# A two-layer hybrid diffusion backbone on one core: half of the weights' low parts go to GpSimd, and the last modulation section is computed by rows on VectorE

## The chip, the cores and the metric

The kernel runs on one core of a Trainium2 chip. The metric is the device time of one execution in microseconds (us), taken as the median of several executions. The core has five engines with their own instruction streams: TensorE (PE, with its weight loads shown as PEld), VectorE (DVE), ScalarE (ACT), GpSimd (POOL) and SyncE (SP), which here only issues DMAs. Each engine runs its instructions in order; semaphores hold an instruction back until what it reads is there and what it overwrites is free.

## The reference

Two layers act on 256 latent tokens and 256 context tokens of width 1024. Each layer computes six modulation sections (shift, scale and gate, twice) from a condition vector, then three token mixers on one normalised input, a gated merge, and a squared-ReLU MLP. In the last layer only the latent tokens go through merge and MLP. Cut to what matters here:

```python
def reference(x, c, ctx, c_ctx, ...):
    h, hc = x, ctx
    for l in range(DEPTH):                                   # DEPTH = 2
        ctx_needed = l < DEPTH - 1
        sh1, sc1, gt1, sh2, sc2, gt2 = modulation(c, ada_w[l], ada_b[l])       # silu(c) @ w + b, in six sections
        sh1c, sc1c, gt1c, sh2c, sc2c, gt2c = modulation(c_ctx, ada_w[l], ada_b[l])
        u  = rms_norm(h,  norm1_g[l]) * (1.0 + sc1)  + sh1
        uc = rms_norm(hc, norm1_g[l]) * (1.0 + sc1c) + sh1c
        ya, yb, yc = ...          # recurrent block, gated linear recurrence, neighbourhood attention, all from u @ w_in[l]
        h = h + gt1 * merge_branches(ya, yb, yc, m_g, w_branch[l], w_out[l])
        h = h + gt2 * sq_relu_ffn(rms_norm(h, norm2_g[l]) * (1.0 + sc2) + sh2, ffn_w1[l], ffn_w2[l])
        if ctx_needed:
            hc = ...              # the same for the context
    return h
```

## The kernel before, in words

The two token streams lie side by side as 512 columns in layer 0. In layer 1 the context is only needed by some projections, and the rest works on 256 columns. Every matmul is done in a split format: a weight piece and its activations are each the sum of a high part and a low part, and three products (high by high, low by high, high by low; L240 to L242, L253 to L255, L272 to L275, L1073 to L1075) stand for one.

A layer has 148 weight pieces of 512 KB, 296 in all, which come in a fixed order. For each piece SP issues one DMA into `raw` (`arriving`, L208 to L212, 3 buffers), ScalarE casts the high part `whi` (L226), and VectorE subtracts it from `raw` to get the low part `wlo` (L227); there are 4 buffers each of `whi` and `wlo`. `fetch` near the end of the kernel starts a piece up to four pieces ahead of its use. The one exception before the change is the very first piece, whose low part is computed on GpSimd by the same line.

The time runs through these stages: a start (0 to about 60 us), four heads of the mixers in layer 0 (to about 390 us), the merge with the output projection (to about 585 us), a norm (`normed`, with lines L461 to L538), the MLP (to about 925 us), the layer boundary with the next norm, four heads in layer 1 (to about 1253 us), the merge of layer 1 (to about 1318 us), its output projection and norm (to about 1350 us) and the last MLP. Within a head the chains of small operations on VectorE and ScalarE (scores, scans, the chunked recurrence with `KK`, `QQ`, `lv`) lie beside the projections `ptok` on PE. In the merge the gates `gt` multiply the projected branches `halves`, and the sum `msum` is split into `mhi` and its low part, which the output projection reads. In a norm the sums of squares `sums` go through PE (`nss`), a short chain on VectorE gives the reciprocal root `r_g` (L531 to L538), PE spreads it (`rst`, L484), and VectorE and ScalarE make the operand `x` (L502 to L506) for the next projections. The residual stream is `h` (L1207).

The modulation sections other than the first two are computed by rows: for a section, 8 DMAs of 512 KB (`arow`) and 16 multiply-and-sum operations on VectorE (`junk`, L395), as lane "X" of the side work. The last section, (1,5), which is the gate after the last MLP, is the exception: `last_modulation` loads 8 blocks (`araw`), PE multiplies them in 32 fp32 matmuls (L419, 64 records in the trace), of which some are placed after output pieces and the rest in the norm of layer 1, and four small matmuls (L428) bring the result into its layout.

GpSimd does little else: constants, a rotary table (`ctab`, L367), and the issue of the DMAs for `bias` and `gw`. Lanes (L101 to L147) decide at each step of the main work which pieces of side work are issued beside it. The instructions of VectorE, ScalarE and GpSimd are put in order by the builder's list scheduler, so an instruction that leaves one engine can change the order of its neighbours.

Of the kernel before, what the change touches and what calls it, by code (L numbers as in the profile page):

```python
# [19 lines left out]
P = 128  # L20
# [7 lines left out]
HB = 64  # L28
# [5 lines left out]
}  # L34
ROW_SECTIONS = ((0, 2), (0, 3), (0, 4), (0, 5), (1, 0), (1, 1), (1, 2), (1, 3), (1, 4))
LAST_SECTION = (1, 5)
MIX_ORDER = ("tok", "ff", "fb", "hq", "ax", "ag", "og")
# [117 lines left out]
def hybrid_kernel(  # L155
    ctx: ExitStack, tc: tile.TileContext, xT, cT, wpack, ada0w, adaw, lastw, prm, lruw, biasd, consts, cs, gfr, masks, out
):
# [17 lines left out]
    def four_k(name, shape=(2, T2), dt=F32):  # L175
        return wk.tile([P] + list(shape), dt, tag="t4", name=name, bufs=N4)

    def psum(tag, name):
        return ps.tile([P, T2], F32, tag=tag, name=name, bufs=PSUM_BUFS[tag])
# [8 lines left out]
    con = cpool.tile([P, P + 1], F32, name="con")  # L188
    sel = cpool.tile([P, 10], F32, name="sel")
    cst = cpool.tile([P, 2, 2, 64], F32, name="cst")  # L190
# [181 lines left out]
    def modulation_rows():  # L372
# [16 lines left out]
        for i, (l, section, k) in enumerate(todo):  # L389
# [16 lines left out]
            yield 2.4, 1 if l or section == 5 else 0  # L406

    def last_modulation():

        l, section = LAST_SECTION  # L410
        raws = []
        for k in range(KD):
            raws.append(four_k("araw", (4, TL)))
            nc.sync.dma_start(out=raws[k], in_=lastw[k].rearrange("p (a b) -> p a b", b=TL))
            yield
        pa = psum("AV", "ada")
        for k in range(KD):
            for g in range(4):
                nc.tensor.matmul(  # L419
                    pa[32 * g:32 * g + 32, :TL], lhsT=cs32[:, k, :], rhs=raws[k][:, g], start=(k == 0), stop=(k == KD - 1)  # L420
                )
            yield
        sb = scr("adasb")[:, :TL]
        nc.vector.tensor_copy(sb, pa[:, :TL])
        yield 0.4, 2
        pt = psum("L", "adat")
        for m in range(2):
            nc.tensor.matmul(pt[:, 8 * m:8 * m + 8], lhsT=sb[:, m * P:(m + 1) * P], rhs=sel[:, 2:], start=True, stop=True)  # L428
        src = pt[:, :16].rearrange("p (m g s) -> p m g s", g=4, s=2)
        b = par(l, "ada_b")[:, section * 8:section * 8 + 8].rearrange("p (g m) -> p m g", g=4)  # L430
        for s in range(2):
            dst = section_of(l, section, s).rearrange("p (g m) -> p m g", g=4)
            nc.vector.tensor_tensor(out=dst, in0=src[:, :, :, s], in1=b, op=ALU.add)
        known.add(LAST_SECTION)

# [676 lines left out]
    def merge_pieces(l):  # L1112
# [73 lines left out]
        def pre_out():  # L1186
            st.u2 = new_u()
            new_sums()
            if l > 0:
                st.late = last_modulation()  # L1190

        def finished(d, s):
            square(d, s, l > 0)
            if l > 0:
                next(st.late)

# [52 lines left out]
    def ffn_pieces(l):  # L1249
# [6 lines left out]
        def open_ffn():  # L1256
            lanes.step("N")
            for _ in range(5):
                next(st.late)
            lanes.step("N")  # L1260
            for _ in range(3):
                next(st.late)
            lanes.start("X", st.late)

# [74 lines left out]
    def start():  # L1339
# [3 lines left out]
        nc.scalar.dma_start(out=con, in_=consts[:, :P + 1])  # L1343
        nc.scalar.dma_start(out=sel, in_=consts[:, P + 1:P + 11])
        for k in range(0, KD, 2):
# [90 lines left out]
        def later():  # L1436

            nc.sync.dma_start(out=prn[1], in_=prm[1][:, :NMOD])
            nc.sync.dma_start(out=cst, in_=cs)
            for l in range(DEPTH):  # L1440
                nc.sync.dma_start(out=gf[l], in_=gfr[l])
                for i in (0, 2):
                    nc.gpsimd.tensor_scalar_mul(gf[l][:, i], gf[l][:, i], 0.125)
            nc.sync.dma_start(out=idh, in_=consts[:, P + 11:])
            mskf = two_k("mskf").rearrange("p (a b) -> p a b", b=HB)[:, :NLEV]
            nc.sync.dma_start(out=mskf, in_=masks)
            nc.gpsimd.tensor_copy(msk, mskf)
# [30 lines left out]
    pos = [0]  # L1478

    def fetch(n):  # L1480
        while len(ready) < n and pos[0] < len(todo):
            l, key = todo[pos[0]]
            ready.append(weights(l, key))
            pos[0] += 1
# [15 lines left out]
def _lay(inputs):  # L1500
# [37 lines left out]
    a["adaw"] = np.concatenate([section(*i).T.reshape(KD, P, D) for i in ROW_SECTIONS])  # L1538
    a["lastw"] = section(*LAST_SECTION).reshape(KD, P, D)

# [36 lines left out]
    i = np.arange(P)  # L1577
    con = np.zeros((P, P + 11 + HB), np.float32)
    con[:, :P] = np.eye(P)
# [13 lines left out]
    a["gfr"] = np.broadcast_to(gr[:, None], (DEPTH, P, 4, 64))  # L1593
    for g in range(4):
        for s in range(2):
            con[:, P + 3 + 2 * g + s] = i == 32 * g + s
    con[:, P + 11:] = i[:, None] % HB == i[None, :HB]
    a["consts"] = con
# [7 lines left out]

_ORDER = ["xT", "cT", "wpack", "ada0w", "adaw", "lastw", "prm", "lruw", "biasd", "consts", "cs", "gfr", "masks"]

# [21 lines left out]
```

## Time and profile before

| | |
|---|---|
| time, median of 3 runs | 1532.23 us (1531.86 to 1532.8) |
| the profiled execution, its own time | 1530.86 us |
| its span in the trace | 1529.1 us |
| PE busy | 1509.4 us (99%) |
| DVE busy | 1167.3 us (76%) |
| ACT busy | 752.8 us (49%) |
| POOL busy | 26.6 us (2%) |
| low parts on DVE (L227, `wlo`) | 295, together 360.3 us |
| rows on DVE (L395, `junk`) | 144, together 173.3 us |

The page gives busy times of each engine over the whole span. A share is an average: PE is nearly always busy, but there are stretches in which it waits for VectorE, and others in which VectorE has time to spare. The stage windows and the timelines show which is which. In a timeline row the columns are start, duration, engine, line, operation, output and inputs, shape and count; in square brackets stands the idle time before the instruction and what ended it. A row with a count over 1 joins several instructions that followed each other.

### The profile page before, as it was taken

Reading aid. Unit: us, or ns where it says so; the run is one execution under the profiler, and the core shown is the slowest. Engines: PE = TensorE matmul, PEld = TensorE weight load, DVE = VectorE, ACT = ScalarE, POOL = GpSimd, SP = SyncE. Lnnn points to the kernel's source line nnn. Section 1 sums busy time; section 2 is a strip of 40 time slices with the busy share of each in tenths; the row PEclk is TensorE's granted clock in tenths of the full one; section 3 lists DMA queues with packets and bytes.
Section 4 is the critical chain, followed back from the end, with each engine's and each line's share of the span. In section 5 each row is a group of like instructions: output and inputs, shape, how many; then the busy total and the mean of one; then the engine's idle time right before and its main releaser. Section 6 shows DMA issues by size and latency. Waiting matters only on the chain.

```text
span 1529.1 us, 22454 instructions
## 1 busy us (share of the span) xinstructions
PE 1509.4 (99%) x8593; PEld 1247.9 (82%) x8594; DVE 1167.3 (76%) x2250; ACT 752.8 (49%) x1285; POOL 26.6 (2%) x57
## 2 busy tenths in 40 slices
PE   9999999999999999999999999999999999989998
PEld 5778787878888889888888888878878888778887
DVE  6777778686478898988695846779678878878886
ACT  3466575656323333532323323576776865444552
POOL 1100000020000000000000000000000000000000
PEclk9999999999999999999999999999999999989999
DMA  9413131222273661555464532414223356635553
GB/s 368 156 42 104 56 104 56 70 76 70 86 259 124 215 213 69 179 192 179 165 206 138 193 111 89 126 62 138 90 70 118 111 179 209 234 132 185 190 191 127
DMA packets 61788, 217.26 MB, mean 142 GB/s; under 512 B 7792, under 2 KB 9456, under 8 KB 61680
## 3 DMA queue, kind: packets, MB, share of 16 engines
q1 hardware_dynamic: 59328, 209.88, 40.1%
q0 software_dynamic: 1648, 5.77, 1.1%
q8 instruction: 68, 1.11, 0.3%
q14 instruction: 40, 0.33, 0.1%
q10 hardware_dynamic: 704, 0.17, 0.1%
HBM read 214.74 MB, written 1.05 MB: 141 GB/s over the span
## 4 chain that ended last, share of the span: by engine, by line
PE 94%; DVE 3%; issue 1%; ACT 1%; DMA 1%; SPq 0%; ACTq 0%
PE pd L240 5%; PE pd L242 5%; PE pd L241 5%; PE pd L275 4%; PE pf L275 3%; PE ptok L1073 3%; PE pf L240 3%; PE pf L241 3%; PE pf L242 3%; PE ptok L1074 3%; PE ptok L1075 3%; PE pg L240 3%; PE pg L242 3%; PE pg L241 3%; PE lv L590 2%; PE pd L273 2%
## 5 line engine op out<-in xcount | busy, mean ns | idle before, releaser
L226 ACT CAST whi<-raw 128x1024 fp32r<-128x1024 f32 x296 | 311.1, 1052 | 446.1 <-PE pd L241 111.8
L227 DVE TENSOR_TENSOR wlo<-raw,whi 128x1024 fp32r<-128x1024 f32 x295 | 360.3, 1224 | 107.0 <-ACT whi L226 101.9
L395 DVE CUSTOM_DVE_ANT_0 junk<-arow,crow 128x1024 bf16<-128x1024 f32 x144 | 173.3, 1220 | 1.5 <-DMA arow<-in_adaw 1.3
L1207 DVE SCALAR_TENSOR_TENSOR h<-pd,mod,h 128x256 f32<-128x256 f32 x160 | 73.7, 482 | 69.7 <-PE pd L242 51.1
L242 PE MATMUL pd<-hhi,wlo 128*128 128x512 f32 (+1 forms) x288 | 105.4, 366 | 0.0
L240 PE MATMUL pd<-hhi,whi 128*128 128x512 f32 (+1 forms) x288 | 105.3, 366 | 0.0
L241 PE MATMUL pd<-hlo,whi 128*128 128x512 f32 (+1 forms) x288 | 105.3, 366 | 0.0
L1073 PE MATMUL ptok<-whi,x 128*128 128x512 f32 (+1 forms) x224 | 86.9, 393 | 1.1 <-DVE h L1207 1.1
L241 PE MATMUL pf<-x,whi 128*128 128x512 f32 x224 | 87.2, 389 | 0.0
L240 PE MATMUL pf<-x,whi 128*128 128x512 f32 x224 | 87.2, 389 | 0.0
L242 PE MATMUL pf<-x,wlo 128*128 128x512 f32 x224 | 87.2, 389 | 0.0
L1074 PE MATMUL ptok<-whi,x 128*128 128x512 f32 (+1 forms) x224 | 85.1, 381 | 0.2 <-DVE x L506 0.2
L1075 PE MATMUL ptok<-wlo,x 128*128 128x512 f32 (+1 forms) x224 | 84.4, 377 | 0.0
L275 PE MATMUL pf<-x,whi 128*128 128x512 f32 x224 | 81.0, 402 | 0.0
L275 PE MATMUL pd<-hhi,whi 128*128 128x512 f32 x224 | 79.9, 396 | 0.0
L240 PE MATMUL pg<-x,whi 128*128 128x512 f32 x192 | 76.2, 397 | 0.0
L242 PE MATMUL pg<-x,wlo 128*128 128x512 f32 x192 | 74.9, 390 | 0.0
L241 PE MATMUL pg<-x,whi 128*128 128x512 f32 x192 | 74.8, 390 | 0.0
L273 PE MATMUL pf<-x,wlo 128*128 128x256 f32 x256 | 67.0, 284 | 0.0
L273 PE MATMUL pd<-hhi,wlo 128*128 128x256 f32 x256 | 66.1, 279 | 0.0
L242 PEld LDWEIGHTS pd<-hhi,wlo 128*128 128x128 f32 x288 | 54.3, 189 | 8.8
L241 PEld LDWEIGHTS pd<-hlo,whi 128*128 128x128 f32 x288 | 54.3, 189 | 8.8
(395 smaller groups left out, 3651.4 us busy)
## 6 DMA issues: line engine op xcount, KB each, us to landing
raw<-in_wpack SPq DMA_DIRECT2D x296, 512.0 KB, 3.3
arow<-in_adaw SPq DMA_DIRECT2D x72, 512.0 KB, 4.7
a<-in_ada0w SPq DMA_DIRECT2D x16, 512.0 KB, 10.3
araw<-in_lastw SPq DMA_DIRECT2D x8, 512.0 KB, 5.7
bias<-in_biasd POOLq DMA_DIRECT2D x7, 512.0 KB, 4.4
h<-in_xT SPq DMA_DIRECT2D x4, 512.0 KB, 5.5
gw<-in_lruw POOLq DMA_DIRECT2D x8, 256.0 KB, 3.0
out<-h SPq DMA_DIRECT2D x8, 128.0 KB, 1.9
```

Of the source, the lines that this page charges most:

```text
L226: nc.scalar.copy(hi, src)
L227: eng.tensor_tensor(out=lo, in0=src, in1=hi.bitcast(F32), op=ALU.subtract)
L240: nc.tensor.matmul(d, lhsT=whi[:, k, :], rhs=xhi, start=(k == 0), stop=False)
L241: nc.tensor.matmul(d, lhsT=whi[:, k, :], rhs=xlo, start=False, stop=False)
L242: nc.tensor.matmul(d, lhsT=wlo[:, k, :], rhs=xhi, start=False, stop=(k == nk - 1))
L273: nc.tensor.matmul(dst[:, :TL], lhsT=wlo[:, k, :], rhs=xk[:, 0], start=False, stop=False)
L275: nc.tensor.matmul(dst, lhsT=whi[:, k, :], rhs=xk, start=False, stop=last)
L395: nc.vector.tensor_tensor_reduce(out=junk, in0=raw, in1=crow[s], scale=1.0, scalar=0.0, op0=ALU.mult, op1=ALU.add, accum_out=section_of(l, ...
L1073: nc.tensor.matmul(dst, lhsT=xhi[:, k, tsl], rhs=whi[:, kk, :], start=(k == 0), stop=False)
L1074: nc.tensor.matmul(dst, lhsT=xlo[:, k, tsl], rhs=whi[:, kk, :], start=False, stop=False)
L1075: nc.tensor.matmul(dst, lhsT=xhi[:, k, tsl], rhs=wlo[:, kk, :], start=False, stop=(k == KD - 1))
L1207: nc.vector.scalar_tensor_tensor(out=h[:, d, sl], in0=p_[:, part], scalar=mods(l, section, s)[:, d:d + 1], in1=h[:, d, sl], op0=ALU.mult, ...
```

## The change

The low part of a weight piece is computed on GpSimd where the piece's position in the order is odd, and also for the first four pieces of the MLP (`f1`) in each layer; all others stay on VectorE. Together with the first piece these are 151 low parts on GpSimd and 145 on VectorE. The modulation section (1,5) joins the others in `ROW_SECTIONS`; `last_modulation`, its input `lastw` and its selection columns go away. Lane "N" (the norm) is then issued in one go when the MLP opens. Line numbers after the change are lower by 1 to 39.

```diff
-ROW_SECTIONS = ((0, 2), (0, 3), (0, 4), (0, 5), (1, 0), (1, 1), (1, 2), (1, 3), (1, 4))
-LAST_SECTION = (1, 5)
+ROW_SECTIONS = ((0, 2), (0, 3), (0, 4), (0, 5), (1, 0), (1, 1), (1, 2), (1, 3), (1, 4), (1, 5))
...
-    def last_modulation():
-
-        l, section = LAST_SECTION
-        raws = []
-        for k in range(KD):
-            raws.append(four_k("araw", (4, TL)))
-            nc.sync.dma_start(out=raws[k], in_=lastw[k].rearrange("p (a b) -> p a b", b=TL))
-            yield
-        pa = psum("AV", "ada")
-        for k in range(KD):
-            for g in range(4):
-                nc.tensor.matmul(
-                    pa[32 * g:32 * g + 32, :TL], lhsT=cs32[:, k, :], rhs=raws[k][:, g], start=(k == 0), stop=(k == KD - 1)
-                )
-            yield
...
             new_sums()
-            if l > 0:
-                st.late = last_modulation()
 
         def finished(d, s):
             square(d, s, l > 0)
-            if l > 0:
-                next(st.late)
...
         def open_ffn():
-            lanes.step("N")
-            for _ in range(5):
-                next(st.late)
-            lanes.step("N")
-            for _ in range(3):
-                next(st.late)
-            lanes.start("X", st.late)
+            lanes.flush("N")
...
+    def low_part_engine(key, i):
+
+        return nc.gpsimd if i % 2 or (key[0] == "f1" and key[1] == 0 and key[2] < 4) else nc.vector
+
     def fetch(n):
         while len(ready) < n and pos[0] < len(todo):
             l, key = todo[pos[0]]
-            ready.append(weights(l, key))
+            ready.append(weights(l, key, eng=low_part_engine(key, pos[0])))
             pos[0] += 1
```

On VectorE in the norm between merge and MLP of layer 0, the order before was this (`r_g` is the reciprocal root, `h` the residual stream, `sums` the sums of squares):

```order
L531 TENSOR_SCALAR r_g_5387<-nss 128x2
L532 TENSOR_SCALAR r_g_5387<-r_g_5387 128x2
L533 TENSOR_SCALAR r_g_5387<-r_g_5387 128x2
L227 TENSOR_TENSOR wlo<-raw,whi 128x1024
L538 SCALAR_TENSOR_TENSOR r_g_5387<-r_g_5387 128x2
L461 TENSOR_TENSOR sums<-sums,sqt 128x256
L538 SCALAR_TENSOR_TENSOR r_g_5387<-r_g_5387 128x2 x3
L1207 SCALAR_TENSOR_TENSOR h<-pd,mod_85,h 128x256
L538 SCALAR_TENSOR_TENSOR r_g_5387<-r_g_5387 128x2 x3
L227 TENSOR_TENSOR wlo<-raw,whi 128x1024
```

Now the same engine has this order at the same place:

```order
L502 TENSOR_SCALAR r_g_5387<-nss 128x2
L503 TENSOR_SCALAR r_g_5387<-r_g_5387 128x2
L504 TENSOR_SCALAR r_g_5387<-r_g_5387 128x2
L509 SCALAR_TENSOR_TENSOR r_g_5387<-r_g_5387 128x2 x2
L432 TENSOR_TENSOR sums<-sums,sqt 128x256
L509 SCALAR_TENSOR_TENSOR r_g_5387<-r_g_5387 128x2 x5
L1174 SCALAR_TENSOR_TENSOR h<-pd,mod_85,h 128x256
```

The low parts have gone from VectorE's chain here; they are on GpSimd, which has no other instruction between them.

On VectorE at the layer boundary, in front of the second norm chain, the order before was this:

```order
L502 SCALAR_TENSOR_TENSOR ut<-h,A_g_8206,rst 128x256
L461 TENSOR_TENSOR sums<-sums,sqt 128x256
L1207 SCALAR_TENSOR_TENSOR h<-pd,mod_85,h 128x256
L506 SCALAR_TENSOR_TENSOR x<-ut,mod_86,x 128x256
L227 TENSOR_TENSOR wlo<-raw,whi 128x1024
L461 TENSOR_TENSOR sums<-sums,sqt 128x256
L227 TENSOR_TENSOR wlo<-raw,whi 128x1024
L531 TENSOR_SCALAR r_g_8388<-nss 128x2
```

Now it is this, with rows of the modulation (L394) among them:

```order
L473 SCALAR_TENSOR_TENSOR ut<-h,A_g_8233,rst 128x256
L432 TENSOR_TENSOR sums<-sums,sqt 128x256
L394 ISA junk,mod_86<-arow,crow 128x1024
L394 ISA mod_86 128x1
L477 SCALAR_TENSOR_TENSOR x<-ut,mod_86,x 128x256
L394 ISA junk,mod_86<-arow,crow 128x1024
L394 ISA mod_86 128x1
L1174 SCALAR_TENSOR_TENSOR h<-pd,mod_85,h 128x256
L226 TENSOR_TENSOR wlo<-raw,whi 128x1024
L432 TENSOR_TENSOR sums<-sums,sqt 128x256
L502 TENSOR_SCALAR r_g_8420<-nss 128x2
```

One low part has gone from this chain, and two row operations have come in ahead of the residual.

On VectorE in the norm of layer 1, the order before was this, up to the chain of the reciprocal root:

```order
L227 TENSOR_TENSOR wlo<-raw,whi 128x1024
L1207 SCALAR_TENSOR_TENSOR h<-pd,mod_86,h 128x256 x2
L227 TENSOR_TENSOR wlo<-raw,whi 128x1024
L461 TENSOR_TENSOR sums<-sums,sqt 128x256
L1207 SCALAR_TENSOR_TENSOR h<-pd,mod_86,h 128x256 x2
L227 TENSOR_TENSOR wlo<-raw,whi 128x1024
L461 TENSOR_TENSOR sums<-sums,sqt 128x256
L1207 SCALAR_TENSOR_TENSOR h<-pd,mod_86,h 128x256
L531 TENSOR_SCALAR r_g_12378<-nss 128x2
```

Now it is this:

```order
L1174 SCALAR_TENSOR_TENSOR h<-pd,mod_86,h 128x256 x3
L432 TENSOR_TENSOR sums<-sums,sqt 128x256 x2
L1174 SCALAR_TENSOR_TENSOR h<-pd,mod_86,h 128x256 x2
L432 TENSOR_TENSOR sums<-sums,sqt 128x256
L1174 SCALAR_TENSOR_TENSOR h<-pd,mod_86,h 128x256 x2
L432 TENSOR_TENSOR sums<-sums,sqt 128x256
L1174 SCALAR_TENSOR_TENSOR h<-pd,mod_86,h 128x256 x2
L502 TENSOR_SCALAR r_g_12403<-nss 128x2
```

No low part stands on VectorE any more in the last steps ahead of the chain.

## Rows read from the trace of the kernel before

**Rows 1.** The page: busy times, and the chain that ended last.
```profile
PE 1509.4 (99%) x8593; PEld 1247.9 (82%) x8594; DVE 1167.3 (76%) x2250; ACT 752.8 (49%) x1285; POOL 26.6 (2%) x57
...
PE 94%; DVE 3%; issue 1%; ACT 1%; DMA 1%; SPq 0%; ACTq 0%
```

**Rows 2.** The page's costliest groups: low parts and rows on DVE.
```profile
L227 DVE TENSOR_TENSOR wlo<-raw,whi 128x1024 fp32r<-128x1024 f32 x295 | 360.3, 1224 | 107.0 <-ACT whi L226 101.9
L395 DVE CUSTOM_DVE_ANT_0 junk<-arow,crow 128x1024 bf16<-128x1024 f32 x144 | 173.3, 1220 | 1.5 <-DMA arow<-in_adaw 1.3
```

**Rows 3.** Timeline of POOL at the start: the one low part on GpSimd.
```profile
11.67 2.34 POOL L227 TENSOR_TENSOR wlo<-raw,whi 128x1024 fp32r<-128x1024 f32 x1 [11.23 <-ACT whi L226]
```

**Rows 4.** Timeline of DVE in the same microseconds.
```profile
11.32 0.17 DVE L342 TENSOR_TENSOR lq<-lq,lz 128x16 f32<-128x16 f32 x1
...
11.73 2.31 DVE L342 TENSOR_TENSOR lq<-lq,lz 128x16 f32<-128x16 f32 x1
```

**Rows 5.** Stage windows: busy time (count) by engine, granted PE clock, DMA share, GB/s.
```profile
60.00:390.00 330.00, 330.00 (x2144) 264.76 (x2143) 236.15 (x474) 208.17 (x388) 10.65 (x21) 1.00 0.22 74
...
625.00:925.00 300.00, 300.00 (x1327) 248.51 (x1325) 223.31 (x349) 92.46 (x121) 0.53 (x1) 1.00 0.50 171
...
1253.00:1320.00 67.00, 65.36 (x385) 54.12 (x386) 57.30 (x115) 37.93 (x75) 0.00 (x0) 1.00 0.63 220
1320.00:1350.00 30.00, 23.02 (x132) 18.83 (x131) 24.31 (x53) 12.80 (x23) 0.00 (x0) 0.83 0.43 140
```

**Rows 6.** Timeline of DVE in the norm of layer 0.
```profile
588.48 1.23 DVE L227 TENSOR_TENSOR wlo<-raw,whi 128x1024 fp32r<-128x1024 f32 x1
```

**Rows 7.** Timeline of PE at the first MLP matmul of layer 0.
```profile
594.34 0.62 PE L253 MATMUL pf<-x,whi 128*128 128x256 f32 x3 [0.49 <-ACT x L505]
```

**Rows 8.** Timeline of DVE at the layer boundary.
```profile
943.68 1.23 DVE L227 TENSOR_TENSOR wlo<-raw,whi 128x1024 fp32r<-128x1024 f32 x1
...
954.94 1.23 DVE L227 TENSOR_TENSOR wlo<-raw,whi 128x1024 fp32r<-128x1024 f32 x1
```

**Rows 9.** Timeline of PE at the layer boundary.
```profile
962.34 0.44 PE L1074 MATMUL ptok<-whi,x 128*128 128x384 f32 x1 [0.20 <-DVE x L506]
```

**Rows 10.** Windows of 10 us in the first head of layer 1.
```profile
1000.00:1010.00 10.00, 10.00 (x54) 7.75 (x52) 8.78 (x26) 7.45 (x16) 0.00 (x0) 1.00 0.29 99
1010.00:1020.00 10.00, 10.00 (x73) 7.58 (x74) 5.04 (x17) 7.88 (x16) 0.54 (x1) 1.00 0.04 9
```

**Rows 11.** Timeline of DVE at the end of the merge of layer 1.
```profile
1309.59 1.22 DVE L227 TENSOR_TENSOR wlo<-raw,whi 128x1024 fp32r<-128x1024 f32 x1 [0.21 <-ACT whi L226]
1310.73 0.42 DVE L230 SCALAR_TENSOR_TENSOR mhi<-msum,mhi 128x256 fp32r<-128x256 f32 x1
1311.06 0.41 DVE L300 TENSOR_TENSOR halves<-halves,pp 128x256 f32<-128x256 f32 x1
...
1312.88 0.42 DVE L230 SCALAR_TENSOR_TENSOR mhi<-msum,mhi 128x256 fp32r<-128x256 f32 x1 [0.48 <-ACT mhi L229]
```

**Rows 12.** Timeline of PE in the norm of layer 1.
```profile
1332.24 0.40 PE L275 MATMUL pd<-mhi,whi 128*128 128x512 f32 x1
1332.57 1.50 PE L419 MATMUL ada<-araw,cs 128*32 128x256 f32 x24
1336.72 0.38 PE L470 MATMUL nss<-con,sums 128*128 128x1 f32 x2 [2.65 <-DVE sums L461]
...
1342.95 0.76 PE L272 MATMUL pf<-x,whi 128*128 128x512 f32 x1 [1.84 <-DVE x L506]
```

**Rows 13.** Timeline of DVE in the same norm.
```profile
1332.86 1.22 DVE L227 TENSOR_TENSOR wlo<-raw,whi 128x1024 fp32r<-128x1024 f32 x1
...
1335.12 1.22 DVE L227 TENSOR_TENSOR wlo<-raw,whi 128x1024 fp32r<-128x1024 f32 x1
```

**Rows 14.** PE lines, by form: line, operation, count, busy us and mean ns.
```profile
L419 PE MATMUL ada<-araw,cs 128*32 128x256 f32 x64 | 4.9, 385 | 0.0
...
L428 PE MATMUL adat<-sel,adasb 128*128 128x8 f32 x4 | 0.5, 235 | 0.0
```

More of the change, by code (lines that the diff above doesn't have):

```diff
@@ L155, in hybrid_kernel @@
 def hybrid_kernel(
-    ctx: ExitStack, tc: tile.TileContext, xT, cT, wpack, ada0w, adaw, lastw, prm, lruw, biasd, consts, cs, gfr, masks, out
+    ctx: ExitStack, tc: tile.TileContext, xT, cT, wpack, ada0w, adaw, prm, lruw, biasd, consts, cs, gfr, masks, out
 ):
@@ L188, in hybrid_kernel @@
     con = cpool.tile([P, P + 1], F32, name="con")
-    sel = cpool.tile([P, 10], F32, name="sel")
+    sel = cpool.tile([P, 2], F32, name="sel")
     cst = cpool.tile([P, 2, 2, 64], F32, name="cst")
@@ L406, in modulation_rows @@
             yield 2.4, 1 if l or section == 5 else 0
-    def last_modulation():
-        l, section = LAST_SECTION
-        raws = []
-        for k in range(KD):
-            raws.append(four_k("araw", (4, TL)))
-            nc.sync.dma_start(out=raws[k], in_=lastw[k].rearrange("p (a b) -> p a b", b=TL))
-            yield
-        pa = psum("AV", "ada")
-        for k in range(KD):
-            for g in range(4):
-                nc.tensor.matmul(
-                    pa[32 * g:32 * g + 32, :TL], lhsT=cs32[:, k, :], rhs=raws[k][:, g], start=(k == 0), stop=(k == KD - 1)
-                )
-            yield
[L423 to L434, printed above, removed]
     known = {(0, 0), (0, 1)}
@@ L1343, in start @@
         nc.scalar.dma_start(out=con, in_=consts[:, :P + 1])
-        nc.scalar.dma_start(out=sel, in_=consts[:, P + 1:P + 11])
+        nc.scalar.dma_start(out=sel, in_=consts[:, P + 1:P + 3])
         for k in range(0, KD, 2):
@@ L1443, in later @@
                     nc.gpsimd.tensor_scalar_mul(gf[l][:, i], gf[l][:, i], 0.125)
-            nc.sync.dma_start(out=idh, in_=consts[:, P + 11:])
+            nc.sync.dma_start(out=idh, in_=consts[:, P + 3:])
             mskf = two_k("mskf").rearrange("p (a b) -> p a b", b=HB)[:, :NLEV]
@@ L1538, in _lay @@
     a["adaw"] = np.concatenate([section(*i).T.reshape(KD, P, D) for i in ROW_SECTIONS])
-    a["lastw"] = section(*LAST_SECTION).reshape(KD, P, D)
     pm = np.empty((DEPTH, P, NPRM), np.float32)
@@ L1577, in _lay @@
     i = np.arange(P)
-    con = np.zeros((P, P + 11 + HB), np.float32)
+    con = np.zeros((P, P + 3 + HB), np.float32)
     con[:, :P] = np.eye(P)
@@ L1593, in _lay @@
     a["gfr"] = np.broadcast_to(gr[:, None], (DEPTH, P, 4, 64))
[L1594 to L1597, printed above, removed]
+    con[:, P + 3:] = i[:, None] % HB == i[None, :HB]
     a["consts"] = con
@@ L1604, in _lay @@
     return {k: np.ascontiguousarray(v) for k, v in a.items()}
-_ORDER = ["xT", "cT", "wpack", "ada0w", "adaw", "lastw", "prm", "lruw", "biasd", "consts", "cs", "gfr", "masks"]
+_ORDER = ["xT", "cT", "wpack", "ada0w", "adaw", "prm", "lruw", "biasd", "consts", "cs", "gfr", "masks"]
 def build(nc, arrays):
```

## The prediction, made before the changed kernel ran

> **What bounds the kernel now.** I read the page first: busy times and the chain that ended last [rows 1]. PE is busy 99% of the span and holds 94% of the chain; VectorE is at 76%, GpSimd at 2%. So PE's own work sets the time, and VectorE matters only where PE waits for it or has it close behind. On average there is room for both edits; the average hides where it is not. The stage windows come second [rows 5]: in the heads of layer 0 VectorE works 236.15 of 330 us (72%) and in the MLP of layer 0 223.31 of 300 us (74%), while PE is busy throughout. In the merge of layer 1 VectorE has 57.30 of 67 us (86%) and PE loses 1.6 us; in the norm behind it PE is busy only 23.02 of 30 us. Timelines of the tight places come last [rows 6 to 13], and the start of the kernel, where GpSimd does once what it is now to do 151 times [rows 3, 4].
>
> **What a low part costs on either engine.** On VectorE it takes 1.22 us [rows 2]. On GpSimd it took 2.34 us, from 11.67 to 14.01 [rows 3]. In the same microseconds VectorE had a subtraction of 128x16, which takes 0.17 us a moment before; the one that began at 11.73 took 2.31 us and ended with GpSimd's [rows 4]. Both of its operands lie in SBUF, as do those of most of VectorE's work here. So while GpSimd computes a low part, VectorE can be held for all of it. A moved part then costs VectorE up to 2.31 - 1.22 = +1.09 us where VectorE has two-operand work ready, and gives 1.22 us where VectorE would have been idle or was reading PSUM. With 150 parts moved the ends are 150 x 1.09 = +163 us and 150 x 1.22 = 183 us less work for VectorE; neither is a change of the span, because PE covers most of both.
>
> The Trainium skill has a rule on this ("SBUF — State Buffer", section "Who interferes with whom"): GpSimd uses VectorE's second pair of SBUF ports, as an exclusive lock; a VectorE instruction with two SBUF inputs and a GpSimd instruction that reads SBUF shut each other out, and the one issued first holds the pair for its whole length. The 2.31 us beside the 2.34 us agree with it. By that rule the sum below stands as it is; with two engines that don't meet, it would be that of the first rival.
>
> **Part one, half of the low parts to GpSimd, stage by stage.**
>
> *MLP of both layers and the gate stretches of layer 0.* PE is busy without a gap and VectorE is at 74% [rows 5]. Every second piece moved adds 1.09 us of hold per two pieces at the worst; in the 300 us there are about 64 pieces, so 32 x 1.09 = 35 us on 223 us, 258 of 300. The buffers of four pieces carry the delay. I take 0; were the cover gone, the price could reach 35 us.
>
> *Norm of layer 0.* Four low parts of the first MLP pieces stood on VectorE; the one at 588.48 lies inside the chain of the reciprocal root, and the other three around it. All go to GpSimd. PE waited 0.49 us at the first matmul [rows 6, 7] and is paced by VectorE and ScalarE behind it. Bounds: all four hidden, 4 x 1.22 = -4.9; all four holding, 4 x 1.09 = +4.4. Two come while VectorE runs `x` without a pause: I take 2 x 1.09, and 0.3 for the rest: +2.5, near the upper end, since the nearest row of a collision [rows 4] is a full hold.
>
> *Layer boundary.* Two low parts, at 943.68 and 954.94, move [rows 8], and PE is paced by `x` from 962.34 on [rows 9]. Behind the first edit alone: -2.4 to +2.2. The second edit puts two row operations ahead of the residual of the second half, 2 x 1.22 = +2.4, and takes one low part away. I take +1.1 for one full hold and +1.9 for the rows, less what the removed part gives back: +3 together, of bounds 0 to +4.8.
>
> *Heads.* Five low parts per head move, 20 in a layer. In layer 0 a head lasts 330 / 4 = 82 us and VectorE has 28% to spare [rows 5], so I take 0 there. In layer 1 it is dense in parts, 8.78 of 10 us in one window and 5.04 in the next [rows 10]; the windows behind these are alike. PE's small matmuls of the recurrence have the chain close behind them. Of 20 moved parts I let 5 or 6 fall into dense stretches and pay in full: 5.5 x 1.09 = +6. The ends are -4 (all hidden, PE gaining nothing it does not wait for) and 20 x 1.09 = +21.8.
>
> *Merge of layer 1.* VectorE is the bound here, with PE waiting for `halves` and `mhi`. Of 18 low parts from 1257 us on, the last at 1309.59, nine move. `halves` reads PSUM and can run beside GpSimd (0.41 us), the others cannot; and there are idles of 0.48 us in which a moved part is free [rows 11]. About five of the nine pay 1.09 - 0.42 = 0.67 us: +3.4, say +3.5. Ends: 9 x 1.22 = -11 if nothing collided, of which PE could use only its 1.6 us of loss [rows 5], and 9 x 1.09 = +9.8.
>
> *Norm of layer 1.* The last projection matmul starts at 1332.24, yet PE waits 2.65 us for `sums` at 1336.72, because two low parts of 1.22 us stand between the last residuals on VectorE [rows 12, 13]. The order shows none there now. That is 2.4 us off the chain, of which I take -2.2 since a late GpSimd part may still hold the chain once. The clock was granted at 0.83 of full over these 30 us [rows 5], which is half for about 10 us (0.17 x 30 / 0.5), the level of 1.2 GHz; PE had been idle in the gap before. A gap that is 2 us shorter remains one, so I leave that fall in place.
>
> **Part two, the last section by rows.** Removed: 4.9 us of matmuls for the section, and 0.5 us for the four small ones [rows 14]. 24 of the 64 ran from 1332.57 on inside the gap in which PE waits anyway [rows 12], and the others between output pieces while PE waits for VectorE. So I count only the four small ones: -0.5, and at most -(4.9 - 1.5) - 0.5 = -3.9. Added: 16 row operations of 1.22 us [rows 2], 19.5 us on VectorE between about 880 us and the boundary, covered by PE (DVE 74% of that stage) but for the two counted there. Eight DMAs of 512 KB replace eight others; the DMA share is 0.50 there [rows 5], so nothing.
>
> **The sum.** 2.5 + 3 + 6 + 3.5 - 2.2 - 0.5 = +12.3 us on the profiled execution's 1530.86 gives 1543.2. That execution lies 1.37 us under the median of the runs shown (1532.23), so 1544.5; I say 1544.
>
> **Rivals.**
>
> 1. *GpSimd fits into VectorE's pauses and VectorE is relieved.* For it: VectorE idles 362 us in the span, and 74% and 72% leave room [rows 5]. Then the norm of layer 1 gives -2.2, the last section up to -3.9, and the loss of PE at the merge 1.6 at most: -7.7 at most, and about -6 with the section at its middle, so 1526. Against it: PE's waits sit where VectorE has no pause [rows 6, 11, 13], and there a hold of 2.31 replaces 1.22.
> 2. *Nothing to measure.* Holds and gains cancel within 3 us: the heads take no loss (-6 from the sum), the merge and the boundary half of theirs (-1.8 and -1.5): +3, or 1535; without the norm of layer 0 as well +0.5, or 1533. For it: PE is busy without a gap in both heads' stages. Against it: the same as against the first.
> 3. *VectorE becomes the bound in the heads of layer 1.* If each of its 20 moved parts pays in full, +21.8 takes the place of +6: 12.3 + 15.8 = +28.1, so 1560. It decides where holds raise VectorE from about 8.8 of 10 us to over 10: two moved parts in a dense window add 2.2 and do so [rows 10]. Against it: the windows between are half empty, and a delay can be caught up there.
> 4. *The other order of holding.* If VectorE gets in first, GpSimd's part waits instead and lands late, and PE waits for `wlo`. Then the price is on PE's weight side, in stretches where pieces are short; a part that comes one VectorE operation of 1.22 us later [rows 2] in each of the 20 places is +24 for +6, so 1563. Against it: four buffers lie between a low part and its use.
>
> **How the numbers follow.** Forecast 0.50 (1537 to 1553 as its own range), rival 1 0.17, rival 2 0.15, rival 3 0.12, rival 4 0.06. The likeliest gives 1544. The range must reach into rivals 1 and 3 so that about 2 in 10 stay outside: 1527 to 1562. 0.2% of the time is 3.1 us, about what can be told from no change here. Faster by more (under 1529.1): rival 1 and a trace of rival 2, 0.18. Within it: most of rival 2, 0.12. Slower: the rest, 0.70.
>
> **What would show it.** In the trace after, each GpSimd low part has 2.3 us, and VectorE rows of 0.4 us with two SBUF operands stretch to up to 2.3 beside it; single-operand rows and those reading PSUM do not. In the norm of layer 1 PE's wait for `sums` falls from 2.65 to about 0.5 us. At the matmuls that stood at 594 and 962 us, PE's waits for `x` grow by 2 to 3 us in all at each place. In the heads of layer 1 PE shows waits for `QQ`, `km` or `x` that it did not have. I am wrong if those rows on VectorE keep their old durations, or if they stretch and PE's stages keep their lengths; then VectorE's pauses are larger where it counts than I read them.

## The result, and the profile after the change

The change makes the kernel slower: 1587.92 us (median of 4 runs, 1586.81 to 1589.49) against 1532.51 us, a ratio of 1.0359 with a 95% interval of 1.0341 to 1.0377. The direction was forecast, the size was not: 55 us instead of 12, and outside the range of 1527 to 1562. (Executions of one kernel lie up to 7 us apart; in the profiles of spare_read, spare_write, two_kept, short_ops and rows_early the clock is granted low for a part of the first 30 us, and some or all of their entry under "start" in the table below comes from that.)

The page after the change answers to [rows 1, 2]: busy times, the chain that ended last, and the groups of low parts and rows (lines left out are marked by dots).

```profile
PE 1521.5 (96%) x8525; PEld 1250.2 (79%) x8526; DVE 1213.4 (77%) x2130; ACT 751.8 (47%) x1285; POOL 410.4 (26%) x207
...
PE 76%; DVE 18%; ACT 4%; issue 2%; DMA 0%; SPq 0%; DVEq 0%; ACTq 0%
...
L226 POOL TENSOR_TENSOR wlo<-raw,whi 128x1024 fp32r<-128x1024 f32 x151 | 385.5, 2554 | 1131.7 <-ACT whi L225 1105.9
...
L226 DVE TENSOR_TENSOR wlo<-raw,whi 128x1024 fp32r<-128x1024 f32 x145 | 180.0, 1242 | 61.4 <-ACT whi L225 60.2
L394 DVE CUSTOM_DVE_ANT_0 junk<-arow,crow 128x1024 bf16<-128x1024 f32 x160 | 215.9, 1366 | 1.4 <-DMA arow<-in_adaw 0.9
```

VectorE has given away 150 low parts, 183 us of work, and taken on 16 rows, 21 us. By this sum it should be busy 1005 us. It shows 1213.4, 46 us more than before: its operations have become longer. The share of the chain that lies on VectorE has grown from 3% to 18%. PE's idle time is 1585.0 - 1521.5 = 63.5 us, against 1529.1 - 1509.4 = 19.7 before, which is 43.8 of the 56 us. The other 12.1 us are time that the trace counts as busy on PE, although 5.4 us of matmuls have gone [rows 14]; a low clock has at most 8.5 us of it (see below), and the rest stays open. These waits of PE in the heads of layer 1 are new:

```profile
PE pr L861 <- DVE lx L226: 6.5, 4, 1.7
PE lv L599 <- DVE QQ L612: 5.5, 4, 1.6
PE sc L760 <- ACT PT L811: 1.4, 1, 1.4
PE pg L271 <- DVE halves L299: 1.1, 2, 0.7
```

These rows give what PE waited for, the total, how often and the longest. The first two come four times each, once in each head. Not one of them names GpSimd's `wlo`; in the whole trace one wait of PE does, of 0.5 us. What they look like, first on GpSimd, then on VectorE, then on PE, in the first head of layer 1 (timelines):

```profile
1025.36 2.38 POOL L226 TENSOR_TENSOR wlo<-raw,whi 128x1024 fp32r<-128x1024 f32 x1 [6.42 <-ACT whi L225]
1054.70 2.85 POOL L226 TENSOR_TENSOR wlo<-raw,whi 128x1024 fp32r<-128x1024 f32 x1 [26.97 <-ACT whi L225]
```

```profile
1026.09 1.93 DVE L946 SCALAR_TENSOR_TENSOR ge<-ge,halves 128x256 f32<-128x256 f32 x1
1027.94 0.41 DVE L772 TENSOR_REDUCE misc<-sc 128x1 f32<-128x256 f32 x1
1028.27 0.68 DVE L226 TENSOR_TENSOR lx<-xc,lx 128x512 fp32r<-128x512 f32 x1
...
1054.62 0.69 DVE L608 TENSOR_TENSOR KK<-KK,aux 128x512 f32<-128x512 f32 x1 [0.32 <-PE lv L561]
1055.23 2.60 DVE L612 TENSOR_TENSOR QQ<-QQ,aux 128x256 f32<-128x256 f32 x1
```

```profile
1029.00 0.74 PE L861 MATMUL pr<-lx,lw 128*128 128x512 f32 x2 [1.65 <-DVE lx L226]
...
1057.97 0.46 PE L599 MATMUL lv<-QQ,KK 128*128 128x128 f32 x2 [1.63 <-DVE QQ L612]
```

The operation on `ge` that starts at 1026.09 ends at 1028.02, after GpSimd's at 1027.74; `lx` comes behind it, and PE waits for `lx`. `QQ` takes 2.60 us, ends at 1057.83 after GpSimd's at 1057.55, and PE waits 1.63 us for it. Before, the same operation took 0.42 us:

```profile
L641 DVE TENSOR_TENSOR QQ<-QQ,aux 128x256 f32<-128x256 f32 x24 | 10.1, 420 | 6.0 <-PE lv L590 3.7 <-PE lv L629 2.3
```

To see where the 56 us of the span lie I paired PE's instructions of both traces by output tile and position, and took the shift of their starts at the stages' edges. Each column is what a stage adds, in us, against the profiled execution before; the experiments stand in the same table. One execution stands behind each line: in layer 0 two_kept and norm_vec have the order of instructions on VectorE that the change has as far as the end of the heads, and their heads read +12.3 and +11.0 beside +9.6, so that entries of this size are good to 2 or 3 us.

```
                start  heads 0  merge 0  norm 0  MLP 0  boundary  heads 1  merge 1  norm 1  MLP 1 |  sum
prediction        -       0        0      +2.5     0      +3.0      +6.0     +3.5     -2.7     0  | +12.3
the change      +1.8    +9.6     +1.5     +4.8     0      +7.0     +24.4     +3.6     +1.8   +1.5 | +56.0
rows_only       -0.6       0     +0.1        0     0      +4.1      -0.1     -0.3     -0.1      0 |  +3.2
gp_only         +1.4    +9.6     +1.5     +4.8     0      +3.0     +22.2     +4.3     +3.6   +1.3 | +51.6
spare_read      +4.0    +9.4     +2.9     +9.5     0      +3.9     +20.2    +12.6     +7.2   +7.7 | +77.4
spare_write     +4.9       0        0     +0.7     0         0         0     +5.4     -1.9      0 |  +9.1
zero_low        -0.6    -0.4     +0.1     -1.0     0      +5.1      +1.8     -3.1     -4.7      0 |  -2.8
two_kept        +3.2   +12.3     +1.6     +4.2     0      +7.9     +11.4     +5.2     +1.0   +1.5 | +48.3
short_ops       +2.1    +7.5     +1.6     +3.9     0      +7.6     +13.0     +0.2     +0.9      0 | +36.7
mlp_only           0    +0.1        0        0     0         0         0     +0.1     -0.2   +0.9 |  +0.8
rows_early      +4.9       0     +0.1     +1.3     0         0      -0.1     -0.3     +1.0      0 |  +6.8
zero_early      -1.1    -0.4     +0.1     -2.2     0      -0.3      +1.9     -2.6     -3.8      0 |  -8.5
norm_vec           0   +11.0     +1.5        0     0      +7.5     +22.7     +3.6     +1.4   +0.9 | +48.6
```

Two further places of the change. In layer 0 half of the heads' loss lies in one spot (+5.0 of 9.6): GpSimd, VectorE and PE there, with VectorE's `KK` before as the first of its rows,

```profile
338.09 2.40 POOL L226 TENSOR_TENSOR wlo<-raw,whi 128x1024 fp32r<-128x1024 f32 x1 [11.94 <-ACT whi L225]
```

```profile
330.02 0.69 DVE L637 TENSOR_TENSOR KK<-KK,blk 128x512 f32<-128x512 f32 x1
...
338.24 2.79 DVE L608 TENSOR_TENSOR KK<-KK,blk 128x512 f32<-128x512 f32 x1
340.96 0.41 DVE L772 TENSOR_REDUCE misc<-sc 128x1 f32<-128x256 f32 x1
```

```profile
344.82 1.12 PE L807 MATMUL tp<-con,s 128*128 128x128 f32 x4 [3.25 <-ACT s L783]
```

The held `KK` has the reduction of the attention scores behind it in VectorE's queue, ScalarE's exponential waits for that, and PE for ScalarE. In the norm of layer 1, which answers to [rows 12, 13], three low parts in a row on GpSimd hold `sums`:

```profile
1380.82 7.42 POOL L226 TENSOR_TENSOR wlo<-raw,whi 128x1024 fp32r<-128x1024 f32 x3 [4.87 <-ACT whi L225]
```

```profile
1381.10 4.94 DVE L432 TENSOR_TENSOR sums<-sums,sqt 128x256 f32<-128x256 f32 x2 [0.72 <-ACT sqt L430]
```

```profile
1391.10 0.58 PE L441 MATMUL nss<-con,sums 128*128 128x1 f32 x2 [4.97 <-DVE sums L432]
```

Two operations that take 0.42 us each took 4.94 together, and PE's wait for `sums` is 4.97 us where it was 2.65 and where the prediction said 0.5.

### The profile page after: what moved, and what is told of

The parts are those of the page before. It is cut to its first block, busy times and chain, and to the rows that moved or that the text cites. A ratio compares the mean times of both kernels' runs of the same rounds, so it can differ in the third digit from the quotient of the medians.

```text
span 1585.0 us, 22365 instructions
## 1 busy us (share of the span) xinstructions
PE 1521.5 (96%) x8525; PEld 1250.2 (79%) x8526; DVE 1213.4 (77%) x2130; ACT 751.8 (47%) x1285; POOL 410.4 (26%) x207
## 4 chain that ended last, share of the span: by engine, by line
PE 76%; DVE 18%; ACT 4%; issue 2%; DMA 0%; SPq 0%; DVEq 0%; ACTq 0%
PE pd L240 4%; PE pd L239 4%; PE pd L241 4%; PE pd L274 3%; PE pf L239 3%; PE pf L241 3%; PE pf L240 3%; PE pg L239 3%; PE pg L240 3%; PE pg L241 3%; PE ptok L1044 3%; PE ptok L1046 2%; PE ptok L1045 2%; DVE wlo L226 2%; PE pd L272 2%; PE pf L274 2%
## 5 line engine op out<-in xcount | busy, mean ns | idle before, releaser
L226 POOL TENSOR_TENSOR wlo<-raw,whi 128x1024 fp32r<-128x1024 f32 x151 | 385.5, 2554 | 1131.7 <-ACT whi L225 1105.9
L226 DVE TENSOR_TENSOR wlo<-raw,whi 128x1024 fp32r<-128x1024 f32 x145 | 180.0, 1242 | 61.4 <-ACT whi L225 60.2
L394 DVE CUSTOM_DVE_ANT_0 junk<-arow,crow 128x1024 bf16<-128x1024 f32 x160 | 215.9, 1366 | 1.4 <-DMA arow<-in_adaw 0.9
```

Source lines behind the costliest of these rows:

```text
L226: eng.tensor_tensor(out=lo, in0=src, in1=hi.bitcast(F32), op=ALU.subtract)
L394: nc.vector.tensor_tensor_reduce(out=junk, in0=raw, in1=crow[s], scale=1.0, scalar=0.0, op0=ALU.mult, op1=ALU.add, accum_out=section_of(l, ...
```

## The experiments

**The rows alone.**

```diff
-        return nc.gpsimd if i % 2 or (key[0] == "f1" and key[1] == 0 and key[2] < 4) else nc.vector
+        return nc.vector
```

> The changed kernel with every low part back on VectorE (but the first): the section by rows alone. Three theories for the 55 us: HOLD (a GpSimd low part holds VectorE's operations with two SBUF operands for its whole length, and PE waits for these), LATE (low parts arrive later from GpSimd and PE waits for them), ORDER (the loss comes from the new order of instructions, the rows at the layer boundary among them). HOLD: within 3 us of the kernel before, 1530 to 1535, with +1 to +2.5 at the boundary and -0.5 or a little more at the norm of layer 1. LATE: the same. ORDER: 5 to 20 us slower than before.

Measured: 1535.34 us against 1530.98, ratio 1.0036 (1.0022 to 1.0050). A little over what HOLD and LATE allow, and below what ORDER asks. In the profile all of it is at the layer boundary (+4.1), where two rows stand ahead of the residual:

```profile
952.13 1.22 DVE L394 CUSTOM_DVE_ANT_0 junk<-arow,crow 128x1024 bf16<-128x1024 f32 x1
953.27 0.09 DVE L394 DVE_READ_ACCUMULATOR2_ANT mod<- 128x1 f32 x1
953.27 0.48 DVE L477 SCALAR_TENSOR_TENSOR x<-ut,mod,x 128x256 fp32r<-128x256 f32 x1
953.67 1.22 DVE L394 CUSTOM_DVE_ANT_0 junk<-arow,crow 128x1024 bf16<-128x1024 f32 x1
954.81 0.09 DVE L394 DVE_READ_ACCUMULATOR2_ANT mod<- 128x1 f32 x1
954.81 0.48 DVE L1174 SCALAR_TENSOR_TENSOR h<-pd,mod,h 128x256 f32<-128x256 f32 x1
```

Before, `h` started at 952.68:

```profile
952.68 0.48 DVE L1207 SCALAR_TENSOR_TENSOR h<-pd,mod,h 128x256 f32<-128x256 f32 x1
```

PE waits 3.8 us for it here, where it waited 1.1 us before; the clock is granted at 0.83 from 950 to 960 us, where it was 1.00, and that is the likely rest of the 4.1 us.

**The low parts alone.** The kernel before with the new `low_part_engine` and nothing else of the change.

> The kernel before with half of the low parts on GpSimd, the last section still by matmuls. HOLD and LATE: nearly the whole loss, 48 to 57 us, 1580 to 1590. ORDER: the loss without what the rows carry, 35 to 50 us.

Measured: 1585.00 us, ratio 1.0359 (1.0342 to 1.0377), +54 us. The low parts carry nearly the whole loss, and stage by stage about the same as in the change, but for the boundary (+3.0 for +7.0) and the norm of layer 1 (+3.6 for +1.8).

**The same GpSimd work for nobody.** VectorE keeps every low part; GpSimd repeats 150 of them.

```diff
-        split(hi, lo, raw, eng=eng)
+        split(hi, lo, raw, eng=nc.vector if eng is nc.gpsimd and key != ("tok", 0, 0) else eng)
+        if eng is nc.gpsimd and key != ("tok", 0, 0):
+            nc.gpsimd.tensor_tensor(out=raw, in0=raw, in1=hi.bitcast(F32), op=ALU.subtract)
```

> The kernel before with every low part on VectorE; for each piece whose low part the change moves, GpSimd does the same subtraction once more behind VectorE's, into the raw buffer, where nobody reads it. VectorE's order is that of before. HOLD: at least as slow as the change, since VectorE is held and not relieved: 50 to 100 us over before, 1582 to 1632. LATE and ORDER: within 3 us of before, 1529 to 1536.

Measured: 1607.47 us, ratio 1.0506 (1.0488 to 1.0525), +76 us. Nobody reads what GpSimd computes here; it only keeps the buffers `raw` and `whi` longer. VectorE's order is that of before in all but 16 of 2250 places, and yet the loss is larger than in the change. LATE and ORDER, which allowed 3 us, fall with this run as causes of the loss. VectorE's busy time is 1390.4 us with the same instructions that took 1167.3: 223 us of holding, 1.5 us for each of the 150.

```profile
PE 1534.6 (96%) x8593; PEld 1254.5 (78%) x8594; DVE 1390.4 (87%) x2250; ACT 752.6 (47%) x1285; POOL 427.6 (27%) x207
```

**GpSimd as busy, but writing only.**

```diff
...
+        if eng is nc.gpsimd and key != ("tok", 0, 0):
+            nc.gpsimd.memset(raw, 0.0)
+            nc.gpsimd.memset(raw, 1.0)
```

> As spare_read, but GpSimd writes the raw buffer twice with a constant and reads nothing. HOLD, where it is the reading that shuts VectorE out: within 3 us of before, and VectorE's rows keep their durations. If any GpSimd access to SBUF holds VectorE: a loss as in spare_read, in proportion to GpSimd's busy time.

Measured: 1536.47 us, ratio 1.0041 (1.0026 to 1.0056). VectorE's operations with two SBUF operands keep their durations. One group in four kernels, the one before, the change, spare_read and spare_write in this order, with mean nanoseconds behind the busy time:

```profile
L461 DVE TENSOR_TENSOR sums<-sums,sqt 128x256 f32<-128x256 f32 x34 | 13.8, 421 | 3.6 <-ACT sqt L459 3.6
```

```profile
L432 DVE TENSOR_TENSOR sums<-sums,sqt 128x256 f32<-128x256 f32 x34 | 31.7, 945 | 6.2 <-ACT sqt L430 6.0
```

```profile
L463 DVE TENSOR_TENSOR sums<-sums,sqt 128x256 f32<-128x256 f32 x34 | 23.2, 699 | 3.0 <-ACT sqt L461 3.0
```

```profile
L464 DVE TENSOR_TENSOR sums<-sums,sqt 128x256 f32<-128x256 f32 x34 | 13.8, 421 | 3.1 <-ACT sqt L462 3.0
```

GpSimd was busy 288 us with these writes, and the heads, the boundary and both MLPs lost nothing. So it is the reading that shuts VectorE's two-operand work out. The expectation of 3 us was missed all the same. Of the 9.1 us in the table, 4.9 lie in the start with its low clock; 5.4 lie in the merge of layer 1, where PE waits 5.4 us for `halves`. The trace points at the `raw` buffers, which come free later there: the issue of their next DMA waits 46.5 us in 11 waits for GpSimd's second write, and ScalarE's cast waits for that DMA, which it did not before (the DMA queue's waits and the engines' from 1255 to 1330 us).

```profile
SPq L211 <- POOL raw L222: 46.5, 11, 7.7
```

```profile
ACT whi L229 <- DMA raw<-in_wpack: 5.7, 4, 2.3
```

This was not tried apart. A part of spare_read's +12.6 in the same stage can have that cause too, since its buffers are also held behind GpSimd.

**The change without the reading.** GpSimd writes zeros in place of its low parts, which leaves out the low parts of 151 pieces.

```diff
+            if eng is nc.gpsimd:
+                nc.gpsimd.memset(lo.bitcast(F32), 0.0)
+            else:
...
```

> The changed kernel in which GpSimd sets its low parts to zero and reads nothing (the low parts of 151 pieces are left out): VectorE's relief and the new order of the change, without the hold. HOLD as the whole of the loss: no slower than rows_only, 1524 to 1535; the relief of the norm of layer 1 (-2.2 in the prediction) shows in its stage. If the new order or the lateness of the low parts carries part of the loss: over 1540.

Measured: 1528.01 us, ratio 0.9972 (0.9962 to 0.9981). The new order, the rows at the boundary (+5.1) and the relief of VectorE together come out faster than before. VectorE is busy 1020.1 us; the change has the same instructions on it and needs 1213.4.

```profile
PE 1506.2 (99%) x8526; PEld 1247.1 (82%) x8526; DVE 1020.1 (67%) x2130; ACT 753.7 (49%) x1285; POOL 168.7 (11%) x207
```

The difference, 193 us or 1.29 us for each moved part, is the holding, and it is what turns -3.5 us into +55. Zeros also wait for no cast and no load, so this run by itself would not tell a hold from a late low part; spare_read, where no low part comes from GpSimd, and the 0.5 us that PE waits for GpSimd's `wlo` in the change do. The norm of layer 1 shows -4.7, the merge of layer 1 -3.1.

**Two pieces of each head kept on VectorE.**

```diff
+        if i >= NPIECE and (key[0] == "fb" or (key[0] == "tok" and key[2] == 3)):
+            return nc.vector
```

> The changed kernel, but in layer 1 the low parts of the pieces tok part 3 and fb of each head (7 in all, two in each head after the first one's tok) stay on VectorE. In the trace of the change these two lie where PE waits in each head, for lx (6.5 us in four heads) and for QQ (5.5 us). HOLD by single collisions: the heads of layer 1 lose 10 to 14 us less, 1574 to 1578. If the loss of the heads is a general lack of VectorE time: 2 to 5 us less, 1583 to 1586.

Measured: 1576.67 us, ratio 1.0288 (1.0265 to 1.0311). With 7 of 20 moved parts taken back the heads of layer 1 lose 11.4 us instead of 24.4. PE's waits for `QQ` are gone, and of those for `lx` one of four is left (1.5 us), that of the first head, whose piece was not among the seven. So more than half of the loss in these heads hangs on two single collisions.

**Each GpSimd low part as two operations of half the width.**

```diff
-            eng.tensor_tensor(out=lo, in0=src, in1=hi.bitcast(F32), op=ALU.subtract)
+            for c in (slice(0, 512), slice(512, 1024)) if eng is nc.gpsimd else (slice(None),):
+                eng.tensor_tensor(out=lo[:, c], in0=src[:, c], in1=hi.bitcast(F32)[:, c], op=ALU.subtract)
```

> The changed kernel with every GpSimd low part as two operations on 512 columns each. HOLD for the length of one GpSimd operation: VectorE gets in between the two, a hold is at most about 1.3 us, and 10 to 30 us of the 55 come back: 1558 to 1578. If what counts is GpSimd's total time at the port: no gain, 1585 to 1595.

Measured: 1566.15 us, ratio 1.0225 (1.0209 to 1.0241): each set against its own runs of the kernel before, 21 us of the 55 come back, although GpSimd's total grows.

```profile
L227 POOL TENSOR_TENSOR wlo<-raw,whi 128x512 fp32r<-128x512 f32 x302 | 444.7, 1493 | 1054.7 <-ACT whi L225 1046.6
...
PE pr L862 <- DVE lx L227: 4.8, 4, 1.3
PE lv L600 <- DVE QQ L613: 2.2, 4, 0.6
```

The wait for `QQ` falls from 1.6 to 0.6 us. It is the length of one GpSimd operation that counts here, and not GpSimd's total.

**GpSimd only in the MLPs**, behind the first group of each, 56 low parts, on the kernel before.

```diff
+        return nc.gpsimd if i % 2 and (key[0] == "f2" or (key[0] == "f1" and key[1] > 0)) else nc.vector
```

> The kernel before with GpSimd computing the odd pieces' low parts only in the MLPs, behind the first group of each (some 56 low parts). HOLD, harmless where PE is the bound and pieces are buffered: within 3 us of before, 1528 to 1534, although VectorE's operations are held there as elsewhere. If each hold costs by itself: 56/150 of the 54 us, 1551.

Measured: 1532.21 us, ratio 1.0006 (0.9996 to 1.0015). VectorE is held here too (`rl` takes 1430 ns where it took 687), and PE hardly sees it: +0.9 us in the last MLP of the profile.

**The rows, done earlier**: rows_only without the row lane's extra pause.

```diff
-            yield 2.4, 1 if l or section == 5 else 0
+            yield 2.4, 0
```

> rows_only without the extra pause of the row lane, so that VectorE has its last row done before the first norm chain of the layer boundary. If the 4.1 us of rows_only at the boundary are the two row operations ahead of the residual: 0 there, and 1529 to 1531.5 in all, the same as before or up to 0.1% faster. If the 20 us of added VectorE work are the cause wherever they lie: 1534 to 1536 again.

Measured: 1533.38 us against 1532.63, ratio 1.0005 (0.9992 to 1.0018). The boundary loses nothing now, as expected; the time is above the expected 1531.5, like that of the kernel before beside it. The +4.9 at the start go with a low clock, as this window shows, whose last three numbers are granted clock, DMA share and GB/s:

```profile
20.00:30.00 10.00, 10.00 (x42) 5.85 (x45) 4.10 (x11) 1.84 (x4) 0.00 (x0) 0.58 1.03 408
```

**zero_low with the rows of rows_early** (the low parts of 151 pieces left out).

> zero_low (GpSimd writes zeros for its low parts and reads nothing; the low parts of 151 pieces are left out) with the row lane of rows_early. The same boundary theory: 4 to 5 us less than zero_low, 1523 to 1525. Else 1527 to 1529.

Measured: 1522.59 us, ratio 0.9935 (0.9914 to 0.9956), a little below the expected 1523, and the boundary at -0.3 us. It leaves work out, so it is no version to use; of those that compute everything none beats the kernel before.

**The first MLP pieces back on VectorE.**

```diff
-        return nc.gpsimd if i % 2 or (key[0] == "f1" and key[1] == 0 and key[2] < 4) else nc.vector
+        return nc.gpsimd if i % 2 and not (key[0] == "f1" and key[1] == 0) else nc.vector
```

> The changed kernel with the low parts of the first eight MLP pieces of each layer on VectorE again. HOLD: the norm of layer 0 gives back most of its 4.8 us and the norm of layer 1 does not get slower, 1580 to 1585. By the prediction's step for the norm of layer 1 (these low parts on VectorE cost 2.2 us there): that stage 2 us slower than in the change, the norm of layer 0 2.5 us faster, 1586 to 1588 in all.

Measured: 1579.57 us, ratio 1.0308 (1.0289 to 1.0327), 8 us less than the change and a little below what HOLD said. The norm of layer 0 is rid of its whole 4.8 us, and the norm of layer 1 is at +1.4, not slower than the +1.8 of the change.

## Why the prediction was wrong in size

**Right:** the mechanism. A GpSimd operation that reads SBUF holds VectorE's operations, and the one row at the start that showed it [rows 3, 4] was enough to forecast a loss. Also right: no loss in the MLP of layer 0 (0 of 0). The merge of layer 1 hits the amount (+3.5 against +3.6) in part by luck. Its relief alone is worth 3.1 us, as zero_low shows, where I allowed 1.6 at most, so the holds cost 6.7 us there; and PE waits 5.6 us for `halves`, which is not held itself (412 ns) but stands in VectorE's queue behind `msum`, `gt` and `mhi`, which are. Rival 4 falls: GpSimd's `wlo` costs PE one wait of 0.5 us.

**The step that failed: the price of a collision, and the cover.** I priced a moved part at 2.31 - 1.22 = 1.09 us, hold less relief, and set VectorE's spare time against it. In VectorE's sum of work the price is even smaller, 1.29 - 1.22 = 0.07 us on average. But in the heads PE does not wait for a sum. It waits for one operation in a chain, `lx` or `QQ`, and the low part that VectorE was spared stood somewhere else. There the full hold counts, up to 2.3 us, less only the slack PE had. short_ops agrees: half as long an operation, half the loss in these heads (13.0 for 24.4).

**Heads of layer 1, +24.4 instead of +6.** Besides the price, I counted 5 or 6 collisions. PE's listed waits in this stretch come to 15.6 us, and 12.0 of them are the two collisions that recur in every head; two_kept takes 13.0 us away by moving just those. The other 8.8 us of the 24.4 are not waits in the trace; up to 1.7 of them are a low clock, and what the rest is stays open. I had the row of PE's small matmuls close behind VectorE, but judged it by VectorE's busy share in windows of 10 us [rows 10], which says nothing on a chain. Rival 3 has nearly the amount (+21.8), but for another reason: it lets VectorE run out of time, and by what was expected of two_kept moving 7 of 20 parts back would then have given 2 to 5 us, not 13.0.

**Heads of layer 0, +9.6 instead of 0.** The same error: "VectorE has 28% to spare" is true, and of no use to a chain that is held; half of the loss is `KK` ahead of the score reduction. The start, the merge of layer 0 and the last MLP, which had no term or 0, add 1.8, 1.5 and 1.5 us.

**Norm of layer 1, +1.8 instead of -2.7.** The reading of [rows 12, 13] was sound, as zero_low shows: without those low parts on VectorE and without reading on GpSimd the stage is 4.7 us shorter, of which up to 1.7 us are a shorter stretch of low clock. The 0.5 us for the last section do not show (rows_only -0.1). But I let "a late GpSimd part" cost 0.2 us, and three of them, 7.42 us, came right onto `sums`. norm_vec shows that on balance nothing was gained by moving them.

**Norm of layer 0, +4.8 instead of +2.5.** All four parts met the chain, where I counted on two: one hold each in `sums`, twice in `r_g`, and in `x`. My upper bound of 4.4 was the right end. Up to 1.7 of the 4.8 us are a fall of the clock that the sum did not have.

**Boundary, +7.0 instead of +3.** gp_only gives +3.0 and rows_only +4.1. I had put 1.1 on the low parts, for one hold, and two were held (`r_g` and `x`). I had put 1.9 on the two rows; in rows_only they delay `h` by 2.1 us and PE waits 3.8 us for it instead of 1.1. rows_early puts the boundary at 0.

**A cost not foreseen: the clock.** Some of PE's longer waits have a fall of the granted clock behind them. Two windows of the change, with PE's wait of 3.25 us in the first and of 3.80 in the second; the clock was 1.00 at the same work before, as the first line shows for the first of them:

```profile
330.00:340.00 10.00, 10.00 (x83) 7.99 (x81) 6.07 (x18) 8.21 (x15) 0.00 (x0) 1.00 0.16 54
...
340.00:350.00 10.00, 6.75 (x28) 5.15 (x29) 4.54 (x13) 5.81 (x12) 0.49 (x1) 0.83 0.17 52
...
970.00:980.00 10.00, 4.70 (x14) 3.43 (x14) 8.02 (x14) 1.67 (x5) 1.28 (x1) 0.83 0.29 95
```

0.83 of ten microseconds at the two levels of 2.4 and 1.2 GHz is 3.4 us at the lower one. Summed over windows of 10 us, the time missing from the full clock is 13.6 us after the change and 5.1 us before. That bounds the clock's share at 8.5 of the 56 us, 1.7 in each of five stages: both layers' heads, both norms between merge and MLP, and the boundary. How much of it PE would have waited anyway is not told apart by these runs.

**On the rule** from the Trainium skill ("SBUF — State Buffer", "Who interferes with whom"): the runs agree that a GpSimd operation that only writes leaves VectorE's two-operand work alone and that one that reads holds it to its end. Its last part, that the one issued first holds the other, is seen on both sides: GpSimd's low parts have a mean of 2.55 us instead of 2.34, and the one at 1054.70, which starts while `KK` has 0.61 us to run, takes 2.85.

## What to carry to other kernels

Before work is moved from VectorE to GpSimd, look not at VectorE's busy share but at each chain in which PE waits for a single VectorE operation with two SBUF operands: a GpSimd operation that reads SBUF can put its whole length into that chain (`QQ` 2.60 us for 0.42). Where PE is the bound and buffers lie between, the move was free here, and gained nothing (mlp_only). If it must be done, short GpSimd operations cost less than long ones (21 of 55 us came back here), and the pieces that collide can be named from the trace and kept.

## What the runs showed of the hardware that was not expected

- I expected rows with one SBUF operand to keep their durations. In the norm of layer 0 after the change one did not: its only tensor operand is `r_g` in SBUF, GpSimd ran from 601.40 to 603.81, and the row took 2.13 us where it took 0.17 before.

```profile
588.06 0.17 DVE L532 TENSOR_SCALAR r_g<-r_g 128x2 int32<-128x2 int32 x1
```

```profile
601.40 2.41 POOL L226 TENSOR_TENSOR wlo<-raw,whi 128x1024 fp32r<-128x1024 f32 x1 [0.48 <-ACT whi L225]
```

```profile
601.69 2.13 DVE L503 TENSOR_SCALAR r_g<-r_g 128x2 int32<-128x2 int32 x1
```

- Such a row is held even by a GpSimd operation that only writes. In spare_write the same two rows of `r_g` take 0.98 us each beside a write of 0.95, first GpSimd, then VectorE:

```profile
608.92 0.95 POOL L221 MEMSET raw<- 128x1024 f32 x1 [8.95 <-issue]
609.93 0.95 POOL L222 MEMSET raw<- 128x1024 f32 x1
```

```profile
608.92 0.98 DVE L535 TENSOR_SCALAR r_g<-r_g 128x2 int32<-128x2 int32 x1
609.93 0.98 DVE L536 TENSOR_SCALAR r_g<-r_g 128x2 int32<-128x2 int32 x1
```

- The row operation `junk`, with both operands in SBUF, is held as well (mean 1366 ns instead of 1220), while `h`, which has one operand in PSUM and one in SBUF, is not (479 ns after, 482 before).
